# Two layers of GLA and RWKV-7: 32 modulation jobs of the second layer change their place

## Chip, cores, metric
The kernel runs on one core of a Trainium2 chip. The metric is the time of one execution on the device in microseconds, as the median of several.

## What is computed
Two transformer layers over 256 tokens of width 2048, in float32. Each layer first makes six vectors of 2048 from the conditioning vector c (shift, scale and gate of the mixer, then of the feed-forward); this is the modulation. Cut to what matters:

```python
cond = jax.nn.silu(c)
for i in range(DEPTH):                      # 2 layers
    mod = cond @ w_ada[i] + b_ada[i]        # 2048 x 12288
    sh1, sc1, gt1, sh2, sc2, gt2 = jnp.split(mod, 6, axis=-1)
    h = rmsnorm(x, g_pre_mix[i]) * (1.0 + sc1) + sh1
    z = h @ w_in[i]
    ...                                     # GLA on one half of z, RWKV-7 on the other
    y = jnp.concatenate([o_gla, o_rwkv], axis=-1) @ w_out[i]
    x = x + gt1 * rmsnorm(y, g_post_mix[i])
    h = rmsnorm(x, g_pre_ffn[i]) * (1.0 + sc2) + sh2
    y = jnp.square(jax.nn.relu(h @ w_ff1[i])) @ w_ff2[i]
    x = x + gt2 * rmsnorm(y, g_post_ffn[i])
```

The modulation depends on c alone, so its place in the kernel is free up to where its values are used.

## The kernel before
Activations stand channel by channel on the partitions, 16 blocks (k-tiles) of 128 channels by 256 tokens. A weight product takes a tile of 1 MB, 128 by 2048, for one block of 128 outputs: `wtile` (line 283) loads it on SP's queue (line 292) into one of the three buffers called raw, and `split` cuts each half into two parts, hi by ScalarE (line 299) and lo by VectorE (line 300), four buffers each. `block_steps` then runs 16 x 3 products (lines 311 to 313: hi with the operand's high part, hi with its low part, lo with its high part).

The modulation isn't done by TensorE. One job, `ada_job(i, j)`, makes 128 of the 12288 outputs of layer i: it loads 1 MB of w_ada on SP's queue (line 255) into a raw buffer of the same three, and one VectorE operation multiplies it with cond and sums (line 256, followed by a short read of the sum). After each 16 jobs `ada_done` adds the bias and folds in a norm weight. Jobs 0 to 15 of a layer are the mixer's shift, 16 to 31 its scale, 32 to 47 its gate, 48 to 63 the feed-forward's shift, 64 to 79 its scale, 80 to 95 its gate.

The stages in order: layer 0's first blocks and mixers (to 583 us), w_out, 16 tiles (to 665), a `boundary` that updates x and makes the next operand, the feed-forward (710 to 1395), a boundary to layer 1, its mixers (1450 to 1935), w_out (to 2020), a boundary, the feed-forward (2050 to 2770), the last update. In a feed-forward four chunks alternate: 16 tiles up (relu, square `sq`, and the operand `hid`, split in two parts) and 16 tiles down; the first seven tiles up are made in the boundary, so that 121 tiles are left.

What sets the order is a list scheduler that goes by priorities and estimated durations, and fixes each engine's queue before the run; nothing is reordered on the chip. `spread(jobs, tiles)` hands out the jobs: with each call of `wtile` it adds len(jobs) / tiles to a credit, and one job is done per whole credit. Jobs left over are done before the next spread begins. `mixers(i)` (line 912) spreads the layer's own remaining jobs over the mixers' weight tiles and w_out's; the words R0, R.3 and Ra of `ORDER` change the rate on the way, Ra spreading what is left over the last 38 tiles of layer 1. `layer(i)` (line 1044) spreads the jobs of the feed-forward:

```python
self.spread([(0, j) for j in range(32, 80)] if i == 0 else [(1, j) for j in range(ADA_FF0, 80)], 58)
...
jobs = [(i, j) for j in range(80, 96)] + [(1, j) for j in range(ADA_FF0) if i == 0]
self.spread(jobs, FF_TILES[i])              # FF_TILES = (118, 100)
```

With ADA_FF0 = 48 layer 0's feed-forward does 16 + 48 = 64 jobs, layer 1's mixers and w_out 32, layer 1's feed-forward 16.

Of the kernel before, what the change touches and what calls it, by code (L numbers as in the profile page):

```python
# [20 lines left out]
KAPPA = 0.6065306597126334  # exp(-0.5)  # L21

# columns of the per-channel parameter table
# [23 lines left out]
KK_SCALE = 65536.0  # keeps the guard of the key norm in Ln's range  # L47
BASE_SET = "natural_log_exp_and_others"
# token-shift columns: blocks of mu
MU_W, MU_A, MU_G, MU_VL, MU_R, MU_K, MU_V = 0, 1, 2, 4, 5, 13, 21  # L50
# blocks of the packed w_in
WB_W, WB_A, WB_G, WB_VL, WB_K, WB_RV, WB_GLA = 0, 1, 2, 4, 5, 13, 29
N_WIN = 53
# blocks that grow k-tile by k-tile while their operand is being made
FIRST = ((WB_W, WB_A, WB_G, WB_G + 1) + tuple(range(WB_K, WB_K + 4)),
         (WB_W, WB_A, WB_G, WB_G + 1, WB_VL, WB_K, WB_K + 1))
NF = 7
# [12 lines left out]
EARLY = ("k01", "k23")  # whose blocks the first layer has at its start  # L70
QUANTUM = 4   # k-tiles of a block in between two steps of the chains
PACE = (1.0, 1.0)    # steps of the chains after each quantum
# the blockwise inverse: its steps per quantum, their size, and how far its priority is put back
# [6 lines left out]
FF_TILES = (118, 100)  # weight tiles of the feed-forward over which the modulation is spread  # L80
ACTIVE = (2, 2)
BACKLOG = (1, 1)
ADA_FF0 = 48  # of the second layer's modulation, done in the first layer's feed-forward
# [5 lines left out]
GROW_LAG = 8  # pairs of k-tiles by which the first blocks' products lag behind their operand  # L89
# [7 lines left out]
def _finish(gen):  # L97
    """runs a generator to its end."""
    while True:
        try:  # L100
            next(gen)
        except StopIteration as e:
            return e.value


class Chains:
    """dependent work of several engines, in steps that are put in between the weight products."""
# [25 lines left out]
    def side_step(self):  # L133
        """one step of the chain with a pace of its own."""
        if not self.side:
            return False
        name, needs, gen = self.side
        if not all(n in self.done for n in needs):
            return False
        try:  # L140
            next(gen)
        except StopIteration:
            self.done.add(name)
            self.side = None
        return True

    def run(self, blocks):
        """the blocks' steps, with the chains' steps in between."""
# [14 lines left out]
class Kernel:  # L163
# [16 lines left out]
    def setup(self, pool):  # L180
        nc, a, c = self.nc, self.a, self.const
        # c on four partitions
# [12 lines left out]
        # silu(c), then on all partitions  # L195
# [9 lines left out]
        # small numbers that guard roots, as bias columns  # L205
# [10 lines left out]
    def constants(self):  # L216
        nc = self.nc
        for i in range(2):
            nc.vector.tensor_scalar(self.dcol(i, "omu"), self.col(i, "mu"), -1.0, 1.0, ALU.mult, ALU.add)
            # halves for sigmoids by tanh; factors left out of the reciprocal roots  # L220
# [21 lines left out]
    def tanh(self, out, in_, bias=0.0, scale=1.0, more=()):  # L242
        """tanh, and back to the tables that the rest of the kernel uses."""
# [7 lines left out]
    def ada_job(self, i, j, single=None):  # L251
        """single: a pool for a job whose outputs are needed at once."""
# [11 lines left out]
    def ada_done(self, i, j0, j1):  # L264
        """bias, and the products with the norms' weights (and with what their roots leave out)."""
# [4 lines left out]
        # shift, scale, gate of the mixer, then of the feed-forward  # L270
# [32 lines left out]
    def block_steps(self, src, xh, xl, order=range(KT), ps=None):  # L303
        """[128 outputs, tokens] = tile^T @ x over 16 k-tiles, in a PSUM tile."""
# [32 lines left out]
    def total(self, tiles):  # L337
        """sum over partitions (and over the tiles) on every partition."""
# [9 lines left out]
    def grow(self, hi, lo, xh, xl, k, m0=0):  # L348
        """one k-tile more for the first blocks."""
# [7 lines left out]
    def first_norm(self, pool, rstd):  # L357
        """the first layer's h, k-tile by k-tile as its modulation comes in, and the first blocks of its product."""
# [17 lines left out]
    def boundary(self, pool, i, y, acc, which, ni, src, out=None):  # L376
        """x += gate * rmsnorm(y), the next operand h = x * rstd * G + sh, and the first blocks of its
        product. These don't wait for rstd: they take u = x * G, and sh in a column of its own, as rstd
        is a factor of whole tokens."""
# [46 lines left out]
    def first_block(self, n, out):  # L426
        """a first block after its factor: on out, without its shift, and the shift."""
# [18 lines left out]
    def x_stat(self, pool, k, ps):  # L446
        """adds the squares of x's blocks k, k + 1 to the sum over channels."""
# [5 lines left out]
    def update(self, i, y, r, which, k):  # L453
        """x += y * r for blocks k, k + 1."""
# [20 lines left out]
    def spread(self, jobs, tiles):  # L475
        """do the ada jobs in between the next weight tiles."""
# [17 lines left out]
    def banks(self):  # L494
        """two banks, one for each head of a pair: their row tiles run side by side."""
        return self.ps2.tile([P, 2, 512], F32, name="p2")

    def gram(self, ps, n, l, r):
        """ps[h, n + c] = l_h^T r_h for both heads and both halves."""
# [9 lines left out]
    def rwkv_gates(self, i, js):  # L509
        """decay gates and rates of the pairs js, and the values' mixing rates."""  # L510
        nc, dcol = self.nc, self.dcol
        got, todo, vms = [], [], []
        for j in js:
# [6 lines left out]
            # th = 2 sigmoid - 1 throughout  # L520
# [15 lines left out]
    def rwkv_keys(self, i, j, k, pk, sg, av):  # L536
        """decays, keys and the strictly causal a.b products of heads 2j, 2j+1."""
        nc, col, dcol = self.nc, self.col, self.dcol
        k2, At, Bt, Kt = (pk[:, n] for n in range(4))
        # twice the running sums of the gate in each half; decay exponents are taken from the middle  # L540
# [19 lines left out]
        # normalized keys  # L560
# [5 lines left out]
        # max(s, g) = relu(s - g) + g  # L566
# [18 lines left out]
    def heads(self, t, n=0):  # L585
        """[128, head, half, 128] view of a bank pair (at block n) or of four units."""
# [652 lines left out]
```

## Time and profile before

| | us |
|---|---|
| median of 3 runs | 2786.74 (2786.28 to 2793.4) |
| span of the profiled execution | 2786.0 |
| TensorE busy (matmul) | 2658.6 |
| VectorE busy | 1997.1 |
| ScalarE busy | 1421.5 |
| the jobs on VectorE (line 256, 192 of them) | 439.0 |

The profiled execution's own time is not printed beside its span; the median lies 0.74 us above the span, which runs from the first to the last instruction. Shares of the whole span mix stages with different limits, so stretches are read one by one. A matmul's end is modelled, and products overlap, so a busy TensorE can still be slowed; its pace is read from the number of products in a stretch.

### The profile page before, as it was taken

How to read it: one execution, taken by the hardware profiler on the slowest of the kernel's cores; microseconds unless marked ns; L12 is line 12 of the kernel's file. 1: busy time of each engine (PE TensorE's matmuls, PEld its weight loads, DVE VectorE, ACT ScalarE, POOL GpSimd, SP SyncE). 2: the span in 40 equal slices, each digit the busy share in tenths (PEclk: the TensorE clock that was granted, in tenths of full speed). 3: DMA queues.
4: the chain of work that ended last, by engine and by line, in shares of the span. 5: the costliest groups of instructions: out<-in, count | busy, mean ns of one | idle time of the engine just before them, and what ended most of it. 6: DMA issues, size and time to landing. Idle time of an engine off the chain costs nothing.

```text
span 2786.0 us, 55551 instructions
## 1 busy us (share of the span) xinstructions
PE 2658.6 (95%) x23388; PEld 2551.7 (92%) x23388; DVE 1997.1 (72%) x2961; ACT 1421.5 (51%) x2357; POOL 59.2 (2%) x153
## 2 busy tenths in 40 slices
PE   5689999999999999999999999999999999999997
PEld 4678888898999999999988889888989999999997
DVE  8997986678867777777777798655785465565655
ACT  3378644445644434434577875444474443443443
POOL 0000000000000000000001000000000000000000
PEclk8799999999999999999999999998999999999999
DMA  9775576576777777777745547654845666666653
GB/s 402 312 278 196 182 279 239 208 271 231 254 287 289 275 284 284 286 281 282 282 176 206 205 154 264 224 175 159 327 157 212 213 213 218 218 213 212 212 184 119
DMA packets 104082, 659.20 MB, mean 237 GB/s; under 512 B 11540, under 2 KB 20884, under 8 KB 32408
## 3 DMA queue, kind: packets, MB, share of 16 engines
q1 hardware_dynamic: 87848, 618.19, 61.5%
q10 hardware_dynamic: 15984, 37.46, 3.7%
q8 instruction: 183, 3.00, 0.4%
q14 instruction: 67, 0.55, 0.1%
HBM read 638.83 MB, written 16.78 MB: 235 GB/s over the span
## 4 chain that ended last, share of the span: by engine, by line
PE 84%; DVE 9%; DMA 3%; ACT 3%; issue 2%; ACTq 0%; POOL 0%; DVEq 0%; SPq 0%
PE pm L311 14%; PE pm L313 14%; PE pm L312 14%; PE px L312 8%; PE px L313 8%; PE px L311 8%; DVE raw L256 3%; DVE lo L300 2%; PE p L504 1%; DMA raw<-in_wout_dram 1%; PE pm L993 1%; PE pm L994 1%; PE px L451 1%; PE pm L995 1%; ACT hi L299 1%
## 5 line engine op out<-in xcount | busy, mean ns | idle before, releaser
L300 DVE TENSOR_TENSOR lo<-raw,hi 128x1024 fp32r<-128x1024 f32 (+1 forms) x792 | 959.7, 1216 | 544.3 <-ACT hi L299 537.8
L299 ACT CAST hi<-raw 128x1024 fp32r<-128x1024 f32 (+1 forms) x792 | 822.3, 1043 | 800.6 <-PE pm L312 356.1
L311 PE MATMUL pm<-hh,hi 128*128 128x256 f32 x2624 | 762.5, 291 | 3.6 <-ACT hi L299 1.5
L313 PE MATMUL pm<-hh,lo 128*128 128x256 f32 x2624 | 750.4, 286 | 3.9 <-DVE lo L300 3.9
L312 PE MATMUL pm<-hl,hi 128*128 128x256 f32 x2624 | 749.9, 286 | 0.0
L311 PEld LDWEIGHTS pm<-hh,hi 128*128 128x128 f32 x2624 | 504.5, 192 | 14.1 <-issue 2.0
L313 PEld LDWEIGHTS pm<-hh,lo 128*128 128x128 f32 x2624 | 504.9, 192 | 8.9 <-DVE lo L300 5.2
L312 PEld LDWEIGHTS pm<-hl,hi 128*128 128x128 f32 x2624 | 505.4, 193 | 4.6 <-issue 1.6
L256 DVE CUSTOM_DVE_ANT_0 raw<-raw,cond 128x2048 f32<-128x2048 f32 x192 | 439.0, 2287 | 38.3 <-DMA raw<-in_ada_dram 37.8
L313 PE MATMUL pm<-hid,lo 128*128 128x256 f32 x1024 | 289.0, 282 | 0.0
L313 PE MATMUL px<-hid,lo 128*128 128x256 f32 x1024 | 288.3, 282 | 0.0
L312 PE MATMUL px<-hid,hi 128*128 128x256 f32 x1024 | 288.2, 281 | 0.0
L312 PE MATMUL pm<-hid,hi 128*128 128x256 f32 x1024 | 288.0, 281 | 0.0
L311 PE MATMUL pm<-hid,hi 128*128 128x256 f32 x1024 | 287.2, 280 | 0.0
L311 PE MATMUL px<-hid,hi 128*128 128x256 f32 x1024 | 287.1, 280 | 0.0
L313 PE MATMUL px<-hh,lo 128*128 128x256 f32 x896 | 253.6, 283 | 0.0
L311 PE MATMUL px<-hh,hi 128*128 128x256 f32 x896 | 253.5, 283 | 0.0
L312 PE MATMUL px<-hl,hi 128*128 128x256 f32 x896 | 253.5, 283 | 0.0
L311 PEld LDWEIGHTS px<-hid,hi 128*128 128x128 f32 x1024 | 194.5, 190 | 0.0
L311 PEld LDWEIGHTS pm<-hid,hi 128*128 128x128 f32 x1024 | 194.4, 190 | 0.0
L313 PEld LDWEIGHTS pm<-hid,lo 128*128 128x128 f32 x1024 | 193.1, 189 | 0.0
L313 PEld LDWEIGHTS px<-hid,lo 128*128 128x128 f32 x1024 | 193.0, 189 | 0.0
(333 smaller groups left out, 4184.4 us busy)
## 6 DMA issues: line engine op xcount, KB each, us to landing
raw<-in_ff_dram SPq DMA_DIRECT2D x242, 1024.0 KB, 4.9
raw<-in_ada_dram SPq DMA_DIRECT2D x192, 1024.0 KB, 6.2
raw<-in_win_dram SPq DMA_DIRECT2D x90, 1024.0 KB, 5.1
raw<-in_wout_dram SPq DMA_DIRECT2D x32, 1024.0 KB, 5.4
raw<-in_ff1s_dram SPq DMA_DIRECT2D x16, 896.0 KB, 4.6
spill<-pk ACTq DMA_DIRECT2D x16, 640.0 KB, 4.1
pk<-spill ACTq DMA_DIRECT2D x16, 640.0 KB, 5.0
raw<-in_w_dram SPq DMA_DIRECT2D x16, 512.0 KB, 10.5
```

What stands on the lines that cost most here:

```text
L256: nc.vector.tensor_tensor_reduce(out=raw, in0=raw, in1=self.cond, op0=ALU.mult, op1=ALU.add, scale=1.0, scalar=0.0, accum_out=self.mod[:, ...
L299: self.nc.scalar.copy(hi, half)
L300: self.nc.vector.tensor_tensor(lo, half, hi.bitcast(F32), op=ALU.subtract)
L311: nc.tensor.matmul(ps, hi[:, n % 8], xh(k), start=n == 0, stop=False)
L312: nc.tensor.matmul(ps, hi[:, n % 8], xl(k), start=False, stop=False)
L313: nc.tensor.matmul(ps, lo[:, n % 8], xh(k), start=False, stop=n == KT - 1)
L451: self.nc.tensor.matmul(ps, self.ones, sq[:, q], start=k + q == 0, stop=k + q == KT - 1)
L504: self.nc.tensor.matmul(v[:, h, n + c], l[hs, cs], r[hs, cs], start=True, stop=True)
L993: nc.tensor.matmul(vps[c], hh[:, kk, cs], hi[:, kq], start=kk == 0, stop=False)
L994: nc.tensor.matmul(vps[c], hl[:, kk, cs], hi[:, kq], start=False, stop=False)
L995: nc.tensor.matmul(vps[c], hh[:, kk, cs], lo[:, kq], start=False, stop=kk == KT - 1)
```

## The change
One number: jobs 48 to 79 of layer 1 (the shift and the scale of its feed-forward) are done in layer 0's feed-forward, which so gets 16 + 80 = 96 jobs over 118 tiles, and `mixers(1)` is left with none. The rest of the diff takes out comments and docstrings.

```diff
-ADA_FF0 = 48  # of the second layer's modulation, done in the first layer's feed-forward
+ADA_FF0 = 80
```

SP's queue in layer 0's feed-forward, third tile onward, before (`in_ff` is a weight tile, `in_ada` a job's load):

```order
L292 DMA raw<-in_ff_dram 128x2048 x2
L255 DMA raw<-in_ada_dram 128x2048
L292 DMA raw<-in_ff_dram 128x2048 x2
L255 DMA raw<-in_ada_dram 128x2048
L292 DMA raw<-in_ff_dram 128x2048 x2
L255 DMA raw<-in_ada_dram 128x2048
```

And now, at the same place:

```order
L292 DMA raw<-in_ff_dram 128x2048
L255 DMA raw<-in_ada_dram 128x2048
L292 DMA raw<-in_ff_dram 128x2048
L255 DMA raw<-in_ada_dram 128x2048
L292 DMA raw<-in_ff_dram 128x2048 x2
L255 DMA raw<-in_ada_dram 128x2048
L292 DMA raw<-in_ff_dram 128x2048
L255 DMA raw<-in_ada_dram 128x2048
L292 DMA raw<-in_ff_dram 128x2048
```

One load of a job stood behind two weight tiles; now one stands behind each of four tiles, and behind two at the fifth.

VectorE's queue there at the end of the first tiles of the up-projection (line 300 is lo, line 256 a job, lines 1070 and 1073 make the operand of the down-projection), before:

```order
L1070 TENSOR_TENSOR sq<-rl 128x256
L300 TENSOR_TENSOR lo<-raw,hi 128x1024
L1073 TENSOR_TENSOR hid<-sq,hid 128x256
L300 TENSOR_TENSOR lo<-raw,hi 128x1024 x2
L256 ISA raw,mod<-raw,cond 128x2048
L256 ISA mod 128x1
L1070 TENSOR_TENSOR sq<-rl 128x256
L300 TENSOR_TENSOR lo<-raw,hi 128x1024
L1073 TENSOR_TENSOR hid<-sq,hid 128x256
```

And now, the same two halves of line 300 behind more jobs:

```order
L1070 TENSOR_TENSOR sq<-rl 128x256
L300 TENSOR_TENSOR lo<-raw,hi 128x1024
L1073 TENSOR_TENSOR hid<-sq,hid 128x256
L256 ISA raw,mod<-raw,cond 128x2048
L256 ISA mod 128x1
L1070 TENSOR_TENSOR sq<-rl 128x256
L256 ISA raw,mod<-raw,cond 128x2048
L256 ISA mod 128x1
L1073 TENSOR_TENSOR hid<-sq,hid 128x256
L300 TENSOR_TENSOR lo<-raw,hi 128x1024 x2
L1070 TENSOR_TENSOR sq<-rl 128x256
L300 TENSOR_TENSOR lo<-raw,hi 128x1024
```

Two jobs now stand with sq and hid ahead of the two lo halves of one tile; before, those halves came first and one job behind them.

VectorE's queue at the start of layer 1's w_out (line 1033 makes its operand, line 1102 sums squares), before:

```order
L300 TENSOR_TENSOR lo<-raw,hi 128x1024
L1033 TENSOR_TENSOR hl<-o,hh 128x256
L256 ISA raw,mod<-raw,cond 128x2048
L256 ISA mod 128x1
L300 TENSOR_TENSOR lo<-raw,hi 128x1024 x2
L1102 TENSOR_TENSOR acc<-acc,sq 128x256
L300 TENSOR_TENSOR lo<-raw,hi 128x1024 x2
```

And now, from the same two operations on:

```order
L300 TENSOR_TENSOR lo<-raw,hi 128x1024
L1033 TENSOR_TENSOR hl<-o,hh 128x256
L300 TENSOR_TENSOR lo<-raw,hi 128x1024 x2
L1102 TENSOR_TENSOR acc<-acc,sq 128x256
L300 TENSOR_TENSOR lo<-raw,hi 128x1024 x2
L1102 TENSOR_TENSOR acc<-acc,sq 128x256
```

The job that stood ahead of the second weight tile's two halves is gone, and so are the others of that stage. On TensorE the small products of the last RWKV pair (lines 654 to 784) stand in the same sequence in both.

## Rows read from the trace of the kernel before

**Rows 1.** Page, busy us, share of the span, count, by engine
```profile
PE 2658.6 (95%) x23388; PEld 2551.7 (92%) x23388; DVE 1997.1 (72%) x2961; ACT 1421.5 (51%) x2357; POOL 59.2 (2%) x153
```

**Rows 2.** Busy us (count): PE, PEld, DVE, ACT, POOL; then PEclk, DMA share, GB/s
```profile
725.00:1395.00 670.00, 670.00 (x5620) 670.00 (x5619) 489.52 (x559) 300.03 (x403) 0.38 (x2) 1.00 0.78 282
2065.00:2765.00 700.00, 700.00 (x5869) 699.93 (x5869) 407.80 (x476) 311.97 (x425) 0.00 (x0) 1.00 0.59 205
...
1450.00:2020.00 570.00, 554.11 (x5379) 507.67 (x5377) 419.11 (x761) 339.63 (x655) 24.28 (x66) 0.98 0.60 213
590.00:660.00 70.00, 69.84 (x580) 69.49 (x579) 58.09 (x62) 31.64 (x48) 0.00 (x0) 1.00 0.93 349
```

**Rows 3.** VectorE by line, 725 to 1395: count, busy us, mean ns, idle before
```profile
L256 DVE CUSTOM_DVE_ANT_0 raw<-raw,cond 128x2048 f32<-128x2048 f32 x63 | 144.2, 2289 | 24.4 <-DMA raw<-in_ada_dram 24.2
L1073 DVE TENSOR_TENSOR hid<-sq,hid 128x256 fp32r<-128x256 f32 x64 | 26.8, 424 | 12.1 <-ACT hid L1072 12.1
```

**Rows 4.** Line 255, the jobs' loads, 1390 to 2060: count, ns, first and last start
```profile
L255 SPq DMA_DIRECT2D raw<-in_ada_dram x32: 327/328/328, 1460.4 to 2007.6; - x32
```

**Rows 5.** Order of time at w_out's start, layer 1: start, us, engine, [idle before]
```profile
1936.95 1.99 ACT L299 CAST hi<-raw 128x1024 fp32r<-128x1024 f32 x2
...
1940.39 2.29 DVE L256 CUSTOM_DVE_ANT_0 raw<-raw,cond 128x2048 f32<-128x2048 f32 x1 [4.67 <-DMA raw<-in_ada_dram]
...
1943.88 0.38 PE L313 MATMUL pm<-hh,lo 128*128 128x256 f32 x1 [1.25 <-DVE lo L300]
```

**Rows 6.** VectorE and TensorE in order of time, layer 1's decay chain
```profile
1676.37 2.29 DVE L256 CUSTOM_DVE_ANT_0 raw<-raw,cond 128x2048 f32<-128x2048 f32 x1
...
1684.73 0.29 PE L859 MATMUL p<-f 64*32 64x32 f32 x14 [1.29 <-issue]
```

**Rows 7.** TensorE's waits, 1450 to 2020: us, times, longest
```profile
PE px L565 <- ACT f L562: 3.4, 1, 3.4
...
PE p L735 <- DVE gm L596: 1.1, 1, 1.1
```

**Rows 8.** Lines 255 and 292, loads, 700 to 1400
```profile
L255 SPq DMA_DIRECT2D raw<-in_ada_dram x64: 327/328/472, 710.9 to 1379.4; - x64
...
L292 SPq DMA_DIRECT2D raw<-in_ff_dram x121: 327/328/395, 706.2 to 1390.8; - x121
```

**Rows 9.** SP in order of time, layer 0's w_out: first and last of 21
```profile
592.43 0.33 SPq L255 DMA_DIRECT2D raw<-in_ada_dram  x1
...
651.70 0.33 SPq L292 DMA_DIRECT2D raw<-in_wout_dram  x1
```

**Rows 10.** ScalarE's casts by line, 590 to 660 and 725 to 1395
```profile
L299 ACT CAST hi<-raw 128x1024 fp32r<-128x1024 f32 x23 | 23.2, 1050 | 22.2 <-DMA raw<-in_wout_dram 20.2 <-PE pm L312 1.8
...
L299 ACT CAST hi<-raw 128x1024 fp32r<-128x1024 f32 x234 | 245.6, 1052 | 291.3 <-PE pm L312 114.2 <-PE px L312 109.9 <-DMA raw<-in_ff_dram 52.3
```

**Rows 11.** VectorE and TensorE in order of time, fifth tile of the feed-forward
```profile
739.16 2.36 DVE L300 TENSOR_TENSOR lo<-raw,hi 128x1024 fp32r<-128x1024 f32 x2
741.61 2.29 DVE L256 CUSTOM_DVE_ANT_0 raw<-raw,cond 128x2048 f32<-128x2048 f32 x1
...
743.83 0.42 DVE L1070 TENSOR_TENSOR sq<-rl 128x256 f32<-128x256 f32 x1
...
746.70 0.28 PE L311 MATMUL pm<-hh,hi 128*128 128x256 f32 x1
```

**Rows 12.** VectorE's waits, 725 to 1395: us, times, longest
```profile
DVE lo L300 <- ACT hi L299: 133.9, 142, 2.6
DVE raw L256 <- DMA raw<-in_ada_dram: 24.2, 27, 2.7
```

**Rows 13.** Busy time by stretch, columns as in rows 2
```profile
1895.00:1900.00 5.00, 4.64 (x51) 4.20 (x52) 5.00 (x8) 2.37 (x6) 0.00 (x0) 1.00 0.38 145
1900.00:1918.00 18.00, 18.00 (x105) 13.10 (x103) 8.10 (x20) 9.11 (x28) 0.00 (x0) 0.53 0.35 126
550.00:580.00 30.00, 28.94 (x217) 23.41 (x218) 23.17 (x46) 18.09 (x45) 0.76 (x1) 1.00 0.37 136
```

## The prediction
> **What bounds the kernel now.** I read the busy lines of the page first: TensorE is busy for 2658.6 of 2786.0 us, VectorE for 1997.1 [rows 1]. An average hides the stages, so I then asked for busy time by stretch. Where the 32 jobs are to go, layer 0's feed-forward (725 to 1395 us), TensorE is busy for 670.00 of 670.00 us at clock 1.00, VectorE for 489.52, DMA at 0.78. Layer 1's feed-forward, with a quarter of the jobs, runs its products at the same pace: 5620 in 670 us against 5869 in 700, 0.119 us each. So the number of modulation jobs beside a weight tile costs TensorE nothing so far [rows 2]. Where the jobs are taken from, layer 1's mixers and w_out (1450 to 2020 us), TensorE is busy for 554.1 of 570 us: all its waiting there is 15.9 us, and no removal of VectorE work can give more than that as long as the clock stays [rows 2]. A reader should see here that the whole gain on offer is 0.6% and that the place that pays is full.
>
> **The change part by part.** A job is one 1 MB load on SP's queue and one 2.289 us VectorE operation with a short read of the sum [rows 3]; from its start to that of the next operation pass 2.22 us (741.61 to 743.83 [rows 11]). 32 jobs are 32 x 2.22 = 71 us of VectorE's queue and 32 loads. With every 16 go up to three operations on 16 columns (bias, norm weight, factor), small beside it, which wait for nothing but the jobs. ScalarE's and GpSimd's queues are not touched. Nothing is added or removed over the kernel; it moves.
>
> *Out of layer 1.* The jobs lie between 1460.4 and 2007.6 us [rows 4]. I look for TensorE waits that end on one of them. The clear one is at w_out's start: VectorE, held by the order of its queue, idles 4.67 us for a job's load, runs the job at 1940.39, and only then makes the two lo halves of a weight tile whose hi halves ScalarE had made from 1936.95 on; TensorE waits 1.25 us for lo, until 1943.88 [rows 5]. The new order has the two lo operations there without the job. -1.25 us; what is late next is the product itself, whose weights are there. The second: a job at 1676.37 sits in the decay chain that feeds line 859, and TensorE waits 1.29 us before line 859 at 1684.73, put down to "issue" [rows 6]. The releaser is not named, so between 0 and -1.3; I take -0.7. The third is 1.1 us before line 735, for VectorE's gm [rows 7], in a stretch where jobs stand in the same queue, though other steps feed gm too: 0 to -1.1, I take -0.4. The largest wait of the stretch, 3.4 us on line 565, is for ScalarE's f of line 562 [rows 7] and stays. Sum: -2.35 us, at most -3.65 from these three.
>
> *Into layer 0's feed-forward.* 64 jobs over 118 tiles become 96. VectorE goes from 489.5 to 489.5 + 71 = 560 of 670 us, 84%; still not full. SP issues 121 + 64 = 185 loads from 706.2 to 1390.8 us now [rows 8]; 217 must fit into the same 684.6 us, one in 3.16 us. All share three raw buffers, so the question is how fast three buffers turn over. The stretch that is nearest is w_out of layer 0 (590 to 660 us), where a job already stands behind each weight tile: 21 loads from 592.43 to 651.70 us, 20 intervals, one in 2.96 us, and TensorE loses 0.16 of 70 us [rows 2, 9]. That is 6% faster than 3.16. But there ScalarE's casts wait for the loads (20.2 of 22.2 us), while in the feed-forward of now they wait for TensorE to free buffers (114.2 + 109.9 of 291.3 us) and for loads 52.3 [rows 10]. So the change eats most of the lead that weights have over TensorE. Where the lead is thinnest I worked out what the new order does: VectorE is nearly gap-free from 723 to 741 us, and ends the first lo of the fifth tile at 739.16 + 2.36 = 741.5. In the new order two more jobs (2 x 2.22) and one more pair sq, hid (up to 2 x 0.42 [rows 3]) stand ahead of it, so it ends at about 741.5 + 4.4 + 0.8 = 746.7; the tile starts at 746.70 and takes lo with its third product, 2 x 0.12 later [rows 11]. That fits by 0.2 us; a job's load that lands 2.7 us late (the longest such wait here [rows 12]) would cost 2.5. Between 0 and +2.5; I take +0.5. For the rest, 32 more places where the VectorE queue, lo and hid behind a job in it, can wait for that job's load: now 27 such waits of 24.2 us cost TensorE nothing [rows 12]. Between 0 and what the slow rival below gives; I take +0.5, since the turnover of 2.96 is nearer than anything else.
>
> Sum against the profiled execution: 2786.0 - 2.35 + 1.0 = 2784.65 us of span; around it lie 2786.74 - 2786.0 = 0.74 us if that execution was a median one. **2785.4 us.** About 0.3%, 8.4 us, is what a measurement of this kernel can tell from no change, so this is none.
>
> **The rivals.** *The clock in layer 1's tail (faster).* From 1900 to 1918 us TensorE's granted clock averages 0.53, so nearly all of it runs at 1.2 GHz instead of 2.4, while it is busy 18.00 of 18.00 us; at full clock the same work is 18 x 0.53 = 9.5 us, so the fall costs up to 8.5 [rows 13]. Ahead of it stand small products of the last RWKV pair and a wait of 0.36 us (4.64 of 5.00 busy) [rows 13]. If lighter VectorE work closes the stretch up so that the clock stays, the time is 2785.4 - 8.5 = 2777. For it: VectorE is busy for 5.00 of the 5.00 us before [rows 13], and what a job takes there goes. Against: the small products stand in the same sequence in the new order. [...] So I leave it a chance of 0.14.
>
> *The supply of weights becomes the bound (slower).* The mechanism is the turnover of the three raw buffers in layer 0's feed-forward; the point from which it decides is 3.16 us per load. In w_out VectorE does one small operation a tile beside lo; in the up-projection it does sq and hid (0.42 us each), with a wait for ScalarE between them of 12.1 / 64 = 0.19 on average [rows 3]. If the second operation and the wait lengthen each turn, that is 0.61 us more per tile, and with 217 / 121 = 1.79 loads per tile 0.34 per load: 2.96 + 0.34 = 3.30. The 57 up-projection tiles carry 57 x 1.79 = 102 loads; 102 x 0.14 = 14 us: 2785.4 + 14 = 2799 us. Against it: these operations can fall into the 133.9 us that VectorE waits for hi now [rows 12], and the down-projections in between let the lead grow again. 0.11.
>
> *Nothing is gained.* The waits in layer 1 pass to the next operand (the weight load instead of lo, ScalarE instead of VectorE), and the feed-forward costs its 1 us: 2787. 0.05, and no different by measurement.
>
> **How the numbers follow.** Forecast 2785.4 with 0.70, nothing gained 0.05, clock 0.14, supply 0.11. Faster by over 0.3% (below 2778.4): the clock case, 0.14. Slower by over 0.3% (above 2795.1): the supply case, 0.11. Same: 0.75. The range reaches from the clock case, 2776, to 2796, the forecast with its bounds in the feed-forward and the lower half of the supply case; it leaves out the rest of that case and a clock that falls more often.
>
> **What would show it.** Right: in 725 to 1395 us TensorE busy without a gap at about 0.119 us a product, VectorE near 84%, DMA near 0.9, ScalarE's casts waiting mostly for loads; no lo wait at w_out's start in layer 1; DMA down there and in the v blocks. Wrong: waits of TensorE for lo or hi in layer 0's up-projection (supply), or a clock row of 1.00 around 1900 us (clock). A new fall of the clock elsewhere in the mixers, which the trace of before cannot exclude, would cost some 8 us and spoil the forecast too.

## The result: slower by 0.54%, and the profile after

The changed kernel takes 2801.69 us in the median (2793.35 to 2808.93, 9 executions), the kernel before 2787.75 us in the same sessions (2781.46 to 2795.99, 9 executions). The ratio is 1.0054, with a 95% interval of 1.0039 to 1.0069. That is about 15 us more, outside the predicted range of 2776 to 2796, and on the other side of the forecast. The time of the supply rival, 2799 us, is 2.7 us away.

First the busy time by stretch, as in [rows 2] (busy us and count of PE, PEld, DVE, ACT, POOL; then PEclk, DMA share, GB/s):

```profile
725.00:1395.00 670.00, 659.65 (x5471) 654.06 (x5469) 539.26 (x602) 281.83 (x389) 1.72 (x2) 1.00 0.90 321
2065.00:2765.00 700.00, 700.00 (x5868) 699.94 (x5868) 413.74 (x483) 319.01 (x438) 0.00 (x0) 1.00 0.60 208
1450.00:2020.00 570.00, 553.66 (x5425) 509.21 (x5424) 362.96 (x714) 350.24 (x674) 24.37 (x66) 0.99 0.46 158
590.00:660.00 70.00, 68.03 (x562) 67.42 (x561) 56.92 (x61) 30.52 (x47) 0.00 (x0) 1.00 0.91 338
```

Layer 0's feed-forward was free of gaps and now isn't: 5471 products instead of 5620 begin in the 670 us, at 0.119 us some 18 us of work that slides back. Layer 1's feed-forward keeps its pace. Who TensorE waits for between 700 and 1440 us (us in total, times, longest):

```profile
PE px L313 <- DVE lo L300: 5.3, 8, 0.8
PE pm L313 <- DVE lo L300: 5.1, 10, 0.8
PE pm L311 <- ACT hi L299: 0.6, 2, 0.4
PE px L311 <- ACT hi L299: 0.3, 1, 0.3
```

Eighteen waits for lo, none over 0.8 us. They sum to 11.3 us, less than what is lost, because the end of the product ahead is modelled. So I take a better measure from the order of time: the first product of the first full tile of this feed-forward, and the first product of the last of its 121 tiles.

```profile
724.52 0.39 PE L311 MATMUL pm<-hh,hi 128*128 128x256 f32 x1
...
1430.76 0.28 PE L311 MATMUL pm<-hid,hi 128*128 128x256 f32 x1
```

Between them lie 706.2 us; in the kernel before they stand at 723.81 and 1410.64, 686.8 us apart, or 5.72 a tile. I call this the **stretch**, and the time from its end to the last instruction the **rest**. The ledger of the two profiled executions is then: start 0.7 later, stretch 19.4 longer, rest 6.7 shorter (1375.4 before, 1368.7 after), together 13.4 of the 13.5 us between the spans of 2786.0 and 2799.5. Of the 120 tiles between these two products 25 are longer, by 0.3 to 1.2 us each: 13 in the up-projections, 8 in the last down-projection, 4 in the other three; the others keep their 5.7. The rest is shorter by less than the fall of the clock that the kernel before had near 1900 us, 8.5 us [rows 13], and that is missing here.

Next, one such turn. VectorE in order of time (start us, us, [idle before, releaser]):

```profile
1327.75 2.28 DVE L256 CUSTOM_DVE_ANT_0 raw<-raw,cond 128x2048 f32<-128x2048 f32 x1
1329.96 0.08 DVE L256 DVE_READ_ACCUMULATOR2_ANT mod<- 128x1 f32 x1
1329.96 0.42 DVE L1070 TENSOR_TENSOR sq<-rl 128x256 f32<-128x256 f32 x1
1330.85 0.43 DVE L1073 TENSOR_TENSOR hid<-sq,hid 128x256 fp32r<-128x256 f32 x1 [0.47 <-ACT hid L1072]
1331.80 2.36 DVE L300 TENSOR_TENSOR lo<-raw,hi 128x1024 fp32r<-128x1024 f32 x2 [0.53 <-ACT hi L299]
1334.08 2.28 DVE L256 CUSTOM_DVE_ANT_0 raw<-raw,cond 128x2048 f32<-128x2048 f32 x1
```

ScalarE in the same turn:

```profile
1330.41 0.41 ACT L1072 CAST hid<-sq 128x256 fp32r<-128x256 f32 x1 [3.75 <-DVE sq L1070]
1330.73 2.00 ACT L299 CAST hi<-raw 128x1024 fp32r<-128x1024 f32 x2
```

And SP's loads:

```profile
1327.86 0.33 SPq L255 DMA_DIRECT2D raw<-in_ada_dram  x1
1330.07 0.33 SPq L292 DMA_DIRECT2D raw<-in_ff_dram  x1
1334.19 0.33 SPq L255 DMA_DIRECT2D raw<-in_ada_dram  x1
```

A tile with a job takes 6.33 us here (1327.75 to 1334.08), against 5.76 that TensorE needs in an up-projection. It is a ring: 2.21 us for the job, 0.89 for sq and the wait for ScalarE's cast of hid, 0.95 for hid and the wait for hi, 2.28 for the two lo. VectorE's job stands ahead of sq; ScalarE's cast of hid waits 3.75 us for that sq, and the hi casts of the next weights stand behind it; lo waits for hi. No load is late in this turn: the hi casts at 1330.73 follow the cast of hid at once, and the job at 1334.08 follows lo. The sequence job, sq, hid, lo, lo stands behind 33 of the 95 jobs between the two products and behind none in the kernel before, where 25 of the 26 jobs with sq right behind have a lo between sq and hid. With the next job right behind it it comes 23 times, and 17 of these turns take 6.33 to 6.38 us.

Each load goes out within 0.1 us after VectorE has freed a raw buffer: 1327.86 after lo, 1330.07 after the job. Counted by buffers, a weight tile holds one from 1330.07 until its lo ends at 1340.5, 10.4 us, and a job holds one from 1327.86 until 1336.4, 8.5 us; three buffers give (10.4 + 8.5) / 3 = 6.3 us a tile. These holds contain the turn's own waits, so this is the same turn counted another way: it says that the buffers are never free, and not whether they or the order of the queues set the pace.

The casts show that loads are late as well, over the whole feed-forward (725 to 1410 us, columns as in [rows 10]):

```profile
L299 ACT CAST hi<-raw 128x1024 fp32r<-128x1024 f32 x231 | 232.0, 1047 | 178.4 <-DMA raw<-in_ff_dram 161.1 <-DVE y L1081 9.5 <-PE px L312 4.8
```

Before, most of their waiting was for TensorE to give hi buffers back [rows 10]; now 161.1 of 178.4 us are for weights that have not landed. The lead is gone. VectorE still has 131 us idle of 670, so it isn't full.

### The profile page after: what moved, and what is told of

Read it like the earlier page. It is cut to its first block, busy times and chain, and to the rows that moved or that the text cites. A ratio compares the mean times of both kernels' runs of the same rounds, so it can differ in the third digit from the quotient of the medians.

```text
span 2799.5 us, 55475 instructions
## 1 busy us (share of the span) xinstructions
PE 2656.7 (95%) x23388; PEld 2545.5 (91%) x23388; DVE 1997.4 (71%) x2961; ACT 1412.4 (50%) x2357; POOL 59.9 (2%) x153
## 4 chain that ended last, share of the span: by engine, by line
PE 70%; DVE 12%; DMA 10%; ACT 4%; issue 3%; ACTq 0%; POOL 0%; DVEq 0%; SPq 0%
PE pm L311 13%; PE pm L313 12%; PE pm L312 12%; PE px L313 6%; PE px L312 6%; PE px L311 6%; DVE raw L256 5%; DMA raw<-in_ff_dram 5%; DVE lo L300 4%; DMA raw<-in_ada_dram 3%; ACT hi L299 2%; PE p L504 1%; PE pm L993 1%; PE px L451 1%; PE pm L994 1%
## 5 line engine op out<-in xcount | busy, mean ns | idle before, releaser
L299 ACT CAST hi<-raw 128x1024 fp32r<-128x1024 f32 (+1 forms) x792 | 811.3, 1040 | 692.1 <-PE pm L312 284.2
```

Source lines behind the costliest of these rows:

```text
L299: self.nc.scalar.copy(hi, half)
```

## The experiments

All times are against the kernel before, run on the same chip in the same session; it had 2784.0 to 2787.0 us in the sessions of the experiments, so kernels of different sessions are compared by their ratios. The edits are shown against the changed kernel (drop's against the kernel before), cut to what matters and without indentation. The first profile of each kernel, as start of the feed-forward, stretch, and rest:

| kernel | median us | ratio, 95% interval | start | stretch | rest |
|---|---|---|---|---|---|
| before | 2787.75 | | 723.8 | 686.8 | 1375.4 |
| changed | 2801.69 | 1.0054, 1.0039 to 1.0069 | 724.5 | 706.2 | 1368.7 |
| half (16 moved) | 2803.92 | 1.0063, 1.0046 to 1.008 | 724.7 | 700.7 | 1378.3 |
| q56 (8 moved) | 2807.08 | 1.0084, 1.0068 to 1.01 | 725.2 | 692.5 | 1379.4 |
| q40 (8 moved back) | 2803.4 | 1.0062, 1.0042 to 1.0082 | 731.9 | 686.3 | 1382.2 |
| sq_act | 2790.65 | 1.002, 1.0003 to 1.0036 | 725.1 | 694.5 | 1367.7 |
| quarterload | 2792.33 | 1.0027, 1.0011 to 1.0043 | 732.4 | 704.7 | 1370.0 |
| shortop | 2794.36 | 1.0041, 1.0027 to 1.0054 | 728.9 | 693.9 | 1367.7 |
| own2 | 2799.17 | 1.0056, 1.0036 to 1.0075 | | | |
| own2late | 2786.43 | 1.0001, 0.9984 to 1.0019 | 732.0 | 686.9 | 1382.5 |
| own1late | 2835.92 | 1.0174, 1.0151 to 1.0197 | 725.3 | 695.4 | 1413.4 |
| own2late48 | 2788.22 | 1.0005, 0.9992 to 1.0018 | 720.9 | 686.8 | 1370.6 |
| own2late56 | 2796.81 | 1.0033, 1.0018 to 1.0048 | 728.7 | 686.8 | 1378.0 |
| drop | 2788.15 | 1.0001, 0.9986 to 1.0017 | 730.8 | 686.8 | 1370.6 |

The stretch is 686.3 to 686.9 us in six of these kernels, and longer in the others; own2 makes the first tiles in another order, so its row has none (it and its edit are told of below). The stretch separates the feed-forward from everything else. Start and rest differ by several us between executions of the same instructions, so a single profile is compared by its stretch, and whole times by medians.

### Fewer jobs moved (half)

```diff
-ADA_FF0 = 80
+ADA_FF0 = 64
```

> Only 16 of the 32 jobs move: layer 0's feed-forward gets 80 jobs over 118 tiles (201 loads), layer 1's mixers and w_out keep 16. The stretch measured here and below runs from the first full tile of layer 0's feed-forward to the start of its last tile: 686.8 us before, 706.2 in the changed kernel. Supply theory (three raw buffers turn over once in 3.3 us beside the up-projection): 201 x 3.3 = 663 < 687, so no loss, stretch 687 to 689. Order theory (a tile with a job takes 6.33 us, because the queues of VectorE and ScalarE wait for each other, against 5.76 for TensorE): 0.68 jobs a tile, mean below 5.76, so only local losses, stretch 688 to 694. Both: time 2783 to 2790, between the two kernels; the loss is not in proportion to the jobs.

2803.92 us, as slow as with all 32, and a stretch of 700.7: both theories fail on the amount. The wait is another one here (725 to 1425 us):

```profile
PE px L311 <- ACT hid L1072: 5.1, 3, 2.8
PE px L312 <- DVE hid L1073: 1.1, 2, 0.7
```

It stands at the change from an up- to a down-projection, where the first product needs hid of the tile just ended. VectorE at the third of these changes:

```profile
1150.31 2.29 DVE L256 CUSTOM_DVE_ANT_0 raw<-raw,cond 128x2048 f32<-128x2048 f32 x1 [0.52 <-DMA raw<-in_ada_dram]
1152.52 0.08 DVE L256 DVE_READ_ACCUMULATOR2_ANT mod<- 128x1 f32 x1
1152.52 0.42 DVE L1070 TENSOR_TENSOR sq<-rl 128x256 f32<-128x256 f32 x1
```

The job waits for its load and holds sq behind it. The two tiles there last 8.9 and 6.7 us instead of 5.7, at the fourth change 9.9 and 8.0. Part of that is the clock, which fell behind both waits; at the fourth change, first the 6 us with the wait, then the 8 us behind it:

```profile
1335.00:1341.00 6.00, 3.94 (x34) 3.74 (x32) 3.98 (x6) 1.56 (x3) 0.00 (x0) 1.00 0.89 329
1341.00:1349.00 8.00, 6.80 (x32) 6.51 (x33) 4.42 (x6) 3.81 (x6) 0.00 (x0) 0.57 0.84 294
```

TensorE is busy for 3.94 of 6 us, and then gets a clock of 0.57. The missing share of the clock comes to 5.1 us over the stretch, which is 13.9 us longer than before; in the changed kernel's stretch the clock stays at 1.00.

### The square on ScalarE (sq_act)

```diff
-nc.vector.tensor_tensor(sq, rl, rl, op=ALU.mult)
+nc.scalar.activation(sq, rl, AF.Square)
```

> The changed kernel with the square of line 1070 made by ScalarE instead of VectorE, so that on ScalarE the cast of hid, and the weight casts behind it, no longer wait for VectorE and the job in its queue. Loads, buffers and jobs are as in the changed kernel. Order theory: the stalls of the up-projections go, those of the last down-projection stay (about 7 us): stretch 692 to 696, time about 2791. Supply theory: 217 loads through three buffers are as slow as they were, VectorE is freed of 0.33 us a tile only: stretch 702 to 706, time 2799 to 2802.

2790.65 us, stretch 694.5: as the order theory said. It takes one link out of the ring, ScalarE's wait for VectorE's sq, and by the ratios, whose intervals lie apart, some 9 of the 15 us with it. (The stretch alone would not show it: the changed kernel's second execution has 696.4, see below.) About 8 us of stalls stay, but not where they were expected (only 1.5 us of them in the last down-projection).

### Own buffers for the jobs (own2, then own2late)

```diff
+if self.own:
+    raw = self.own.tile([P, D], F32, name="own", bufs=OWN)   # OWN = 2
 self.spread(jobs, FF_TILES[i])
+self.own = pool if i == 0 else None
```

> The changed kernel with two buffers of their own for the jobs of layer 0's feed-forward, so that the three raw buffers serve weights alone. Supply theory: the stalls go, stretch 687 to 690, time about 2784. Order theory: weights land early, but the casts stand behind VectorE's job as before, 6.33 us for each tile with a job: stretch 699 to 705, time 2795 to 2801.

The time, 2799.17 us, looks like the order theory, but the trace puts the loss elsewhere. From the first down-projection on the feed-forward has no stall: 792.0 to 1427.3 is 635.4 us, before 775.5 to 1410.6, 635.1. The loss lies ahead of it. SP took loads for the new, empty buffers into layer 0's w_out:

```profile
578.33 15.15 SPq L260 DMA_DIRECT2D own<-in_ada_dram  x4
```

and TensorE waited there for the weights behind them (580 to 660 us):

```profile
PE pm L318 <- DVE lo L305: 8.9, 3, 7.4
```

The order theory isn't refuted by this, though, since the order didn't stay. With buffers of their own for the jobs the scheduler put a lo between sq and hid:

```profile
889.38 2.29 DVE L261 CUSTOM_DVE_ANT_0 own<-own,cond 128x2048 f32<-128x2048 f32 x1 [0.76 <-DMA own<-in_ada_dram]
891.60 0.08 DVE L261 DVE_READ_ACCUMULATOR2_ANT mod<- 128x1 f32 x1
891.60 0.42 DVE L1076 TENSOR_TENSOR sq<-rl 128x256 f32<-128x256 f32 x1
891.94 1.22 DVE L305 TENSOR_TENSOR lo<-raw,hi 128x1024 fp32r<-128x1024 f32 x1
893.08 0.42 DVE L1079 TENSOR_TENSOR hid<-sq,hid 128x256 fp32r<-128x256 f32 x1
893.50 1.23 DVE L305 TENSOR_TENSOR lo<-raw,hi 128x1024 fp32r<-128x1024 f32 x1
```

The two waits for ScalarE are gone, and from the start of the job to the end of the second lo it takes 5.35 us, against 6.41 above. The sequence job, sq, hid, lo, lo stands nowhere in own2, nor in the versions that follow from it.

To keep these loads out of w_out, the next version lets the first use of each buffer wait for the feed-forward's operand:

```diff
+if self.fresh:
+    self.fresh -= 1
+    nc.gpsimd.tensor_copy(raw[:, 0:1], self.hh[:, KT - 1, 0:1].bitcast(F32))
```

> As the kernel with two buffers of their own for the jobs, but their first use waits for the operand of the feed-forward (a tiny GpSimd copy of one column of it into each), so that no load of these jobs can be taken ahead into layer 0's w_out. Buffer theory (the jobs' hold on the three raw buffers is the whole cost in the feed-forward): no loss ahead of the feed-forward, stretch 686 to 689, and layer 1's gain of 3 to 10 us is left: time 2776 to 2784, below the kernel before. Rival (the 32 loads and VectorE operations cost their time wherever they stand, own buffers only move the loss): 10 us or more lost between 583 us and the end of the feed-forward, time 2793 to 2800.

2786.43 us, ratio 1.0001: the whole loss is gone, with all 96 jobs and 217 loads in the feed-forward. The stretch is 686.9, and the casts wait for TensorE again. The feed-forward by stretch:

```profile
725.00:1395.00 670.00, 669.92 (x5615) 669.71 (x5615) 555.85 (x621) 298.71 (x407) 0.39 (x2) 1.00 0.88 334
```

Its casts, 725 to 1410 us (line 307 is line 299 of before; the edit moves the line numbers):

```profile
L307 ACT CAST hi<-raw 128x1024 fp32r<-128x1024 f32 x240 | 252.0, 1050 | 320.5 <-PE px L320 133.7 <-PE pm L320 132.9 <-DVE lo L308 26.8
```

VectorE at 555.85 us and the queue at 0.88 (334 GB/s, more than the 321 with stalls) do not bound it. Freed buffers and another order came together here, so this run doesn't tell which of them took the loss away. The expected gain below the kernel before did not come.

### One own buffer (own1late)

> The same with one buffer of its own instead of two. A job's load then can't be issued before the job ahead of it is done: one job per 5.4 us of landing and 2.2 us of VectorE's operation is 7.6 us, against one job per 1.23 tiles or 7.1 us wanted. Buffer theory: VectorE waits for some of the loads, the weights have three buffers still: stretch 687 to 694, time 2778 to 2789. Rival as above: 2793 to 2800.

The edit is OWN = 1. 2835.92 us: neither theory saw this. The stretch is 695.4, but a job must now be done before the next one's load goes out, and the last are not done when the feed-forward ends. Three of them on VectorE, at the end, 7.3 us apart:

```profile
1503.45 2.29 DVE L264 CUSTOM_DVE_ANT_0 own<-own,cond 128x2048 f32<-128x2048 f32 x1 [1.83 <-DMA own<-in_ada_dram]
...
1510.80 2.29 DVE L264 CUSTOM_DVE_ANT_0 own<-own,cond 128x2048 f32<-128x2048 f32 x1 [5.05 <-DMA own<-in_ada_dram]
...
1518.12 2.29 DVE L264 CUSTOM_DVE_ANT_0 own<-own,cond 128x2048 f32<-128x2048 f32 x1 [5.01 <-DMA own<-in_ada_dram]
```

TensorE waits for what is made from their sums at layer 1's start (1425 to 1560 us):

```profile
PE pm L319 <- DVE der L285: 31.1, 1, 31.1
```

My own sum, 7.6 us a job against 7.1 wanted, pointed this way, to a lateness of 48 us over 96 jobs; it was more, since the 96 jobs started 8.4 us apart in the mean (719.9 to 1518.1 us). That the time is longer by about as much as the 48 us is chance. I had looked at the weights alone.

### A quarter of the load (quarterload) and of the operation (shortop)

```diff
+short = i == 1 and 48 <= j < 80
+w = 512 if short else D
-nc.sync.dma_start(out=raw, in_=self.a["ada"][i, j])
+nc.sync.dma_start(out=raw[:, :w], in_=self.a["ada"][i, j][:, :w])
-    out=raw, in0=raw, in1=self.cond, ...
+    out=raw, in0=self.cond if short else raw, in1=self.cond, ...
```

> The changed kernel with only a quarter of the load (128 x 512) for the 32 moved jobs; their VectorE operation keeps its length (it takes cond for both operands, so these 32 outputs of the modulation are not the reference's). Buffers and order are as in the changed kernel, 24 MB less are moved in layer 0's feed-forward. Supply theory, with the landing of the loads as what is slow: stretch 687 to 692, time about 2786. Order theory: the turns that wait for no load stay at 6.33 us, stretch 697 to 703, time 2792 to 2798.

2792.33 us, stretch 704.7 in the profiled execution (its slowest): by the ratio some 7 to 8 us of the 15 are left when 24 MB are not moved. The interval overlaps the changed kernel's a little, and VectorE's order is another from 1176 us on (the sequence job, sq, hid, lo, lo 23 times instead of 33), so that less transfer helps is likely and not shown.

For shortop the load stays and in0, in1 and out are cut to 512 columns for the 32 jobs.

> The changed kernel with VectorE's operation of the 32 moved jobs cut to a quarter of its columns (512 of 2048, some 0.6 us instead of 2.29; these 32 outputs are not the reference's). The loads keep their size and number, and go through the same three raw buffers. Theory that VectorE's turn (lo, job, sq, hid) is what holds the buffers too long: about 1.6 us less in the turns of a third of the jobs, the other two thirds keep 6.3 us: stretch 689 to 698, time 2786 to 2795. Rival (transfers, 217 MB through a queue that is busy for 0.90 of the time): no change, 703 to 707, time 2798 to 2803.

2794.36 us, stretch 693.9, in the range that the theory of VectorE's turn gave. But the interval (1.0027 to 1.0054) overlaps the changed kernel's, and 693.9 is close to the 696.4 of its second execution: the 4 us that seem to be gone are not shown.

### Layer 1 alone (drop) and the buffers alone (own2late48)

```diff
-self.spread(... else [(1, j) for j in range(ADA_FF0, 80)], 58)
+self.spread(... else [], 58)
+nc.vector.tensor_copy(self.mod[:, 1, 48:80], self.mod[:, 0, 48:80])
+self.ada_done(1, 48, 64)
+self.ada_done(1, 64, 80)
```

> The kernel before with jobs 48 to 79 of layer 1 left out altogether: their 32 outputs are copied from layer 0's, so the output is not the reference's. Layer 0's feed-forward is as before; only layer 1's mixers and w_out lose the jobs. Theory that the clock's fall at the end of layer 1's mixers goes with the jobs: 2775 to 2780, granted clock near 1.00 in the last 40 us of the mixers. Rival (the fall is there in one execution and not in another, and the jobs cost only waits of 1 to 3 us): 2783 to 2785.

Ratio 1.0001 (0.9986 to 1.0017): leaving the 32 jobs out gains nothing that can be measured, at most 0.14% or 4 us. So the change had at most that to win.

> The kernel before (48 jobs of layer 1 in layer 0's feed-forward) with the two late buffers for the jobs of that feed-forward. Buffer theory: the stretch was without a stall before, so nothing is gained, 2784 to 2788. If this is faster than the kernel before by 3 us or more, own buffers bring something else than the freed turnover, and the gain of the same buffers in the changed kernel isn't layer 1's alone.

Ratio 1.0005, stretch 686.8: the buffers alone bring nothing. What own2late wins over the changed kernel is the stalls. As in all versions with own buffers, VectorE's order in the feed-forward isn't quite that of the kernel beside it.

### The same kernels again (before_again, after_again)

> The kernel before once more, for a second profile of the same instructions. If the clock's fall at 1900 us belongs to the 32 jobs, it is there again, 18 us at about 0.53. If it is there in one execution and not in another, as the profiles of the other kernels suggest, it may be missing, and the start of layer 0's feed-forward may lie up to 8 us away from 723.8.

> The changed kernel once more. If the stalls of layer 0's feed-forward come from the order of the queues, they stand at nearly the same tiles and the stretch is 704 to 708 again; if they come from the transfers of one execution, it differs by more than 3 us. Layer 1's clock as said of the kernel before.

The second execution of before had a span of 2795.5 us: start 731.3, stretch 686.8, rest 1377.3, and the clock fell again near 1900 us. Layer 0's w_out has the same order in all these kernels but own2 and, by a few small steps, drop, and yet the feed-forward starts between 720.9 and 732.4 us. The second one of the changed kernel had 2794.3: start 728.9, stretch 696.4, rest 1369.1. The stretch differs by 9.8 us from the first, with stalls at other tiles: the order makes the places where a late load hurts, and the landings of one execution decide which of them do. Of the 23 turns like the one above 21 take 6.33 to 6.39 us here, and the up-projections lose 4.6 us instead of 9.7: the ring is there in both executions, and does not make the whole loss.

Start and rest differ mostly by the clock. If the missing share of the granted clock is summed over the rest and taken off, the kernel before has 1349.1 and 1351.5 us, the changed kernel 1351.3 and 1349.7, drop 1350.9. I call this the rest at full clock; with 32 jobs in layer 1 or none it is the same within 2.5 us. Ahead of the feed-forward the same sum is 34.1 and 39.3 us in the two executions of before, 5 of the 7.5 us between their starts.

### Around 48 jobs (q56, q56_again, q40, own2late56)

```diff
-ADA_FF0 = 80
+ADA_FF0 = 56    # q40: 40; own2late56: 56 with the two late buffers
```

> Only 8 of the 32 jobs move: 72 jobs over the 118 tiles of layer 0's feed-forward, 193 loads, one in 3.56 us. Theory that the mean rate of loads decides (the prediction's point of 3.16 us a load): no stall, stretch 687 to 689, time 2784 to 2788. Theory that single places decide, where a job whose load is late stands on VectorE ahead of sq, hid or lo: some of the 14 us that 16 jobs cost, stretch 689 to 698, time 2788 to 2798.

> The kernel with 8 moved jobs once more, for a second profile: its first was the fastest of six executions, with a stretch of 692.6 us. Theory that its loss lies in the feed-forward, in another amount in each execution: a slower execution has a stretch of 698 to 708. Rival (it lies in layer 1, whose 24 jobs stand in another order): the stretch is 690 to 695 again and the time from its end to the end of the kernel is 1380 us or more, against 1375 to 1377 of the two profiles of the kernel before.

2807.08 us: with three shared buffers the fewest moved jobs cost the most. The second profile has a span of 2809.6 us and a stretch of 703.8, against 692.5: its loss is in the feed-forward, in another amount each time; a rest at full clock of 1355.0 and 1355.7 us says that layer 1 has a share of some 5 us too. Two tiles after an up-projection take 8.9 and 8.1 us, as in half. The mean rate is no measure, since 193 loads (one in 3.56 us) cost as much as 217.

> 56 jobs of layer 1 in layer 0's feed-forward (8 moved) with two late buffers of their own. Theory that the jobs' hold on the three raw buffers makes their loads late: stretch 687 to 689, time 2783 to 2789. Rival (an order of VectorE's queue that is bad in itself): the loss of the kernel with 8 moved jobs stays, 2798 to 2808.

The stretch is 686.8: own buffers take the feed-forward's loss away here too, and neither this kernel nor q56 has the sequence job, sq, hid, lo, lo. So here late loads through the shared buffers are the nearest cause, though VectorE's order differs in other places. 2796.81 us, ratio 1.0033, so that 9 us stay; some 6 of them are layer 1's with its 24 jobs in another order (rest at full clock 1356.8).

> Eight jobs fewer in layer 0's feed-forward than before (56 over 118 tiles, 177 loads, one in 3.88 us), eight more in layer 1's mixers and w_out. Theory that the loss grows with jobs from some number on: no stall in the feed-forward, stretch 687, and layer 1 loses 0 to 2 us: time 2783 to 2789. Rival (the number of before fits the plan, and any other number brings jobs with late loads to the wrong places): stretch 690 to 700, time 2790 to 2805.

2803.4 us, and each theory is half right: the feed-forward has no stall (686.3), and layer 1 with 40 jobs loses (rest at full clock 1359.9, some 9 us more). Its worst wait (1457 to 2028 us) is the one of [rows 5], grown:

```profile
PE pm L313 <- DVE lo L300: 7.3, 5, 5.2
```

So with shared buffers 48 is the largest of the tried numbers without stalls in the feed-forward, and layer 1 is as fast with 32 jobs as with none, but not with 24 or 40.

## Why the prediction was wrong, step by step

- **What bounds the kernel.** Right that the place that pays is full, and that little is to be had where the jobs are taken from: leaving them out altogether gains nothing measurable (drop). But "the number of jobs beside a weight tile costs TensorE nothing so far" was read from 64 and 16 jobs, and ends above 64: at 72 there are stalls.
- **w_out's lo wait, -1.25.** Right. VectorE in the new order, with no job ahead of lo:

```profile
1953.03 2.36 DVE L300 TENSOR_TENSOR lo<-raw,hi 128x1024 fp32r<-128x1024 f32 x2 [2.31 <-ACT hi L299]
```

  The stage by stretch, in which TensorE has no gap:

```profile
1935.00:2020.00 85.00, 85.00 (x700) 83.06 (x699) 42.08 (x53) 40.19 (x64) 3.22 (x16) 1.00 0.50 178
```

- **Line 859, -0.7, and gm, -0.4.** Wrong in sign. These waits (1450 to 2040 us) are longer than in [rows 6, 7]:

```profile
PE p L735 <- DVE gm L596: 2.8, 2, 1.9
PE p L859 <- issue: 2.5, 1, 2.5
```

  They are the same in the second execution. A wait whose releaser wasn't named, and one with other steps that feed it, were no gains to count. Of layer 1's whole term of -2.35 nothing is left: without the fall of the clock [rows 13] the rest of before would be 1375.4 - 8.5 = 1366.9 us, against 1368.7 in the changed kernel, and at full clock the two executions of each agree, as told above.
- **The start of the feed-forward, +0.5.** Right: the fifth tile took 6.06 us in the one and 6.18 in the other execution instead of 5.76.
- **The rest of the feed-forward, +0.5: the step that failed.** It measured 19.1 and 9.2 us in the two executions. I had worked out two turnovers, 2.96 us a load from w_out and 3.30 for the up-projection, and took the first "since the turnover of 2.96 is nearer than anything else". The second was the one with sq, hid and their waits in it, and the ring measured 6.33 / 2 = 3.17 without a wait for a load; turns with such a wait took up to 7.9 us, 3.9 a load. In w_out the casts waited for loads and a little for TensorE [rows 10], not behind a step that waits for VectorE's job. The reason against the rival, that these operations fit into VectorE's 133.9 us of waiting for hi, failed as well: that waiting was slack of the lead, and it shrank with the lead, to 83.9 us.
- **The supply rival.** Its place was right. Its size (+14 us for 102 loads of the up-projections; about 15 in the median) is in part luck: the up-projections lost 9.7 and 4.6 us in the two executions, the remainder lies in the down-projections. Its mechanism, that the three raw buffers turn too slowly, isn't separated from the order of the queues at 96 jobs: sq_act takes most of the loss away with three buffers and all the loads, own2late all of it with two more buffers and another order. At 72 jobs own2late56 speaks for the buffers. Its point of decision was wrong. By a mean rate of 3.16 us a load 193 loads should have been free and were not, and 217 with own buffers are. The late tiles stand in runs of tiles with a job each, and at the changes from up to down, where a job with a late load stands ahead of sq. A chance of 0.11 was far too low for a case that had the nearer row on its side. The Trainium skill ("Trainium Kernel Development and Optimization", section "Best Practices") says that consistent bubbles can mean that the memory on the chip ran out. Here the memory had room, for two more buffers fitted, and the bubbles came at other tiles in each execution; with these two buffers the 19.4 us went to 0.1.
- **"The down-projections let the lead grow again."** In part. Those of the first three chunks have 4 late tiles of 48. In the fourth one ScalarE's square of y waits for VectorE as hid does, and 8 of its tiles are late in the first execution, though only one in the second. Four hi and four lo buffers also keep the cast weights at two tiles, so a long calm stretch saves up no more than these and what stands in raw.
- **The clock rival.** Its event happened in both profiled executions of the changed kernel, and gave back part of the loss; whether through the change is open. In the last 20 us of layer 1's mixers the changed kernel kept its clock (1916 to 1936 us):

```profile
1916.00:1936.00 20.00, 19.64 (x191) 16.32 (x189) 14.79 (x34) 12.34 (x35) 0.00 (x0) 1.00 0.32 115
```

  own2late, whose layer 1 has the same instructions in the same order, lost it there:

```profile
1910.00:1940.00 30.00, 29.64 (x200) 23.31 (x199) 15.71 (x36) 13.13 (x37) 0.00 (x0) 0.66 0.19 68
```

  and own2late48, with the 32 jobs in place, kept it:

```profile
1880.00:1920.00 40.00, 39.65 (x352) 33.61 (x351) 29.02 (x54) 21.85 (x53) 0.00 (x0) 1.00 0.41 151
```

  The fall comes in some executions and not in others. Of the 17 profiles it stands right ahead of w_out in six of the eight with jobs in that stage and in one of the nine without, which speaks for the rival. The mean granted clock of all executions speaks against it: 0.980 for the 12 of drop as for the 29 of before in that session, at a ratio of 1.0001. So a tie to the jobs is neither shown nor excluded. The idle time ahead is 0.35 or 0.36 us in all 17. The Trainium skill ("TensorE: Matmul & The Clock Gate", section "HAM oscillation — how this bites in real kernels") lays a lowered clock to waits for data between bursts of products; these are several times as long as the 0.36 us here, so that rule doesn't account for the fall. What does was not found.

**What stays open.** How the loss at 96 jobs divides between the ring and late loads: a run with more buffers and the changed kernel's own order is missing. Why 8 moved jobs cost more than 32 in the median: the places at the changes from up to down are worse there, layer 1 adds some 5 us, and the clock has a share (a mean of 0.978 in q56's six executions, 0.981 in the 16 of before in that session, by my estimate up to 8 us of 2800), but the parts were not followed through the executions. And what in layer 1's order with 24 or 40 jobs costs 5 to 9 us was read only from its waits.

No version that was run is faster than the kernel before. own2late equals it.

## What to carry to other kernels

When work is moved beside a full engine, add up one turn of the engine that does it, in the order of its queue and with its waits for the other engine: 2.21 + 0.89 + 0.95 + 2.28 = 6.33 us a tile against 5.76 says more than 84% of VectorE or a mean rate of loads. When an edit cures a stall, look whether the scheduler changed the order along with it. Take the turnover from a stage with the same in-order steps behind the moved one; slack that is spent as waiting for a lead isn't free time. And try the neighbours of a number on both sides: 40 and 56 cost 0.6% and 0.8% where 48 was the plan's best.

## What was not expected of the hardware

Behind the same order of mixers and w_out the feed-forward of layer 0 began between 720.9 and 732.4 us, and the executions of the kernel before in one session lay between 2778.66 and 2799.53 us (29 of them), so a ledger from one profile can be off by 10 us in either direction. And a longer landing need not cost anything: with own buffers the jobs' loads took 7.4 us to land in the median, with shared ones 5.8, and only the shared ones made TensorE wait. The weights' loads beside them went the other way, 5.4 us with own buffers and 6.5 with shared ones.
